# The feed-forward products of a two-layer block as 2x2 blocks with seven products, block sums on GpSimd

## The chip, the cores and the metric

The kernel runs on one core of one Trainium2 chip, in one launch. The metric is the device time in microseconds, as the median of three runs; lower is better. The engines are TensorE (PE; its weight loads are PEld), VectorE (DVE), ScalarE (ACT), GpSimd (POOL) and SyncE (SP), which issues the DMAs.

## What is computed

One sequence of 512 tokens with 1024 features passes two layers of a first block and then one layer of a second block (a sparse attention over compressed, selected and windowed keys). A layer of the first block has a mixer (mLSTM and sliding-window attention) and a feed-forward part, which is what is changed here. All values are float32.

```python
D_MODEL, SEQ, DEPTH, D_FF = 1024, 512, 2, 4096

def sqrelu_mlp(h, w_up, w_down):
    return jnp.square(jax.nn.relu(h @ w_up)) @ w_down

for l in range(DEPTH):
    h = rmsnorm(x, norm_mix_g[l])
    x = x + mixer_block(h, ...)
    h = rmsnorm(x, norm_mlp_g[l])
    x = x + sqrelu_mlp(h, w_up[l], w_down[l])
```

## The kernel before

Activations lie feature-major: a tile holds 128 features on the partitions and all 512 tokens along the free dimension, so 1024 features are eight tiles. To keep float32 accuracy, each operand is split in two parts of the type fp32r, a high part `h` (a rounded copy, made on ScalarE) and a low part `l` (the value less `h`, made on VectorE). A product of two operands is three matmuls: `h*h`, `l*h` and `h*l` (`mm3`).

`gemm` makes one output tile of 128 features and 512 tokens: `wload` fetches one column tile of the weights (128 x 1024, 512 KB) into `raw`, makes `wh` on ScalarE and `wl` on VectorE, and 8 k tiles x 3 matmuls of 512 columns add up in one PSUM bank (tag `g`, four banks). The weights are the stationary operand of each matmul.

In `mlp` the feed-forward part goes in four quarters `qr`. In each, eight up tiles are made from the normed input `xs` (already split, with the norm's gain), then eight down tiles from the eight new hidden tiles `hid`, which are added to the residual `x` in SBUF. The norm's scale per token, `Rb`, multiplies an up tile on its way out of PSUM, in the same instruction as the relu:

```python
self.stt(z, ps, 0.0, Rb, ALU.max, ALU.mult)
self.nc.scalar.activation(z, z, AF.Square)
hid.append(self.split(z, None, "hid"))
```

After the last quarter, `done` is called for each tile: it adds the square of the tile to the statistics of the next norm (`stat_add`: square on ScalarE, sum on GpSimd), spills the tile to DRAM and splits it for the next stage (`prep`). In the second layer a second scaled copy and a second sum of squares are made.

The order of the work is a plan. Every instruction is first recorded in program order (`Recorder`); `issue` then runs a list schedule over the five engines with modelled durations (`cost`), latencies between engines (`LAT`) and the slots of the tile pools, and emits the instructions in that order. Each engine takes its own queue in order. The model has no term for two engines that hinder each other. Pools: `u` (128 x 512 tiles, 79 slots), `raw`, `wh` and `wl` (3 slots each), PSUM banks `g`, `a`, `o`. All instructions are emitted from one line (L306), so the profile's groups are told apart by the tiles' names.

## Time and profile before

| | |
|---|---|
| Runs, median (lowest to highest of 3) | 2189.11 us (2189.09 to 2190.42) |
| Profiled execution, span from first to last instruction | 2187.0 us |
| The time less the span | 2.1 us |
| TensorE busy | 2143.8 us (98%) |
| VectorE, ScalarE, GpSimd busy | 1382.8, 1061.7, 456.8 us |
| Granted clock of TensorE, mean | 0.996 |

The span is that of one profiled execution, the median that of unprofiled runs; what lies around the span is their difference. Matmuls are pipelined: a record's duration is longer than the distance between two starts, so a pace is read from the starts.

### The profile page before, as it was taken

Reading aid. Unit: us, or ns where it says so; the run is one execution under the profiler, and the core shown is the slowest. Engines: PE = TensorE matmul, PEld = TensorE weight load, DVE = VectorE, ACT = ScalarE, POOL = GpSimd, SP = SyncE. Lnnn points to the kernel's source line nnn. Section 1 sums busy time; section 2 is a strip of 40 time slices with the busy share of each in tenths; the row PEclk is TensorE's granted clock in tenths of the full one; section 3 lists DMA queues with packets and bytes.
Section 4 is the critical chain, followed back from the end, with each engine's and each line's share of the span. In section 5 each row is a group of like instructions: output and inputs, shape, how many; then the busy total and the mean of one; then the engine's idle time right before and its main releaser. Section 6 shows DMA issues by size and latency. Waiting matters only on the chain.

```text
span 2187.0 us, 28119 instructions
## 1 busy us (share of the span) xinstructions
PE 2143.8 (98%) x10389; PEld 1766.4 (81%) x10389; DVE 1382.8 (63%) x2591; ACT 1061.7 (49%) x2066; POOL 456.8 (21%) x502
## 2 busy tenths in 40 slices
PE   8999999999999999999999999999999999999998
PEld 6778788887888888887878888788888798888887
DVE  6688995444343445678897445434435677888886
ACT  4466773234232334456675223422324456687783
POOL 3133551012000002014454002000000514232310
PEclk9999999999999999999999999999999999999999
DMA  5223223432333333322322333233333343222321
GB/s 163 77 64 91 75 71 102 130 97 92 97 99 97 97 97 116 97 78 77 88 70 80 112 124 97 87 96 97 98 96 116 97 152 102 69 76 67 90 78 58
DMA packets 72425, 206.10 MB, mean 94 GB/s; under 512 B 9760, under 2 KB 18592, under 8 KB 72288
## 3 DMA queue, kind: packets, MB, share of 16 engines
q1 hardware_dynamic: 72288, 204.31, 30.8%
q8 instruction: 81, 1.33, 0.2%
q14 instruction: 56, 0.46, 0.1%
HBM read 197.86 MB, written 6.42 MB: 93 GB/s over the span
## 4 chain that ended last, share of the span: by engine, by line
PE 79%; DVE 11%; ACT 4%; POOL 3%; issue 2%; DMA 0%; SPq 0%; DVEq 0%; POOLq 0%; ACTq 0%
PE g L306 62%; PE gt L306 6%; DVE L L306 3%; PE O L306 2%; PE PT L306 2%; PE S L306 2%; PE go L306 2%; DVE wl L306 1%; DVE hal L306 1%; PE num L306 1%; ACT L L306 1%; POOL vd L306 1%; ACT wh L306 1%; PE ST L306 1%; POOL sq L306 1%
## 5 line engine op out<-in xcount | busy, mean ns | idle before, releaser
L306 ACT ACTIVATE wh<-raw 128x1024 fp32r<-128x1024 f32 (+2 forms) x344 | 355.4, 1034 | 792.3 <-PE g L306 603.0
L306 PE MATMUL g<-xgh,wh 128*128 128x512 f32 x1512 | 595.6, 394 | 1.9 <-ACT xgh L306 1.7
L306 PE MATMUL g<-xgl,wh 128*128 128x512 f32 x1512 | 595.5, 394 | 0.1
L306 PE MATMUL g<-xgh,wl 128*128 128x512 f32 x1512 | 594.3, 393 | 0.8 <-POOL wl L306 0.8
L306 DVE TENSOR_TENSOR wl<-raw,wh 128x1024 fp32r<-128x1024 f32 (+2 forms) x327 | 406.9, 1245 | 118.0 <-ACT wh L306 117.2
L306 PEld LDWEIGHTS g<-xgh,wh 128*128 128x128 f32 x1512 | 284.7, 188 | 55.4 <-ACT xgh L306 2.7
L306 PEld LDWEIGHTS g<-xgh,wl 128*128 128x128 f32 x1512 | 284.7, 188 | 55.3 <-POOL wl L306 1.2
L306 PEld LDWEIGHTS g<-xgl,wh 128*128 128x128 f32 x1512 | 284.6, 188 | 53.8 <-DVE xgl L306 1.2
L306 POOL TENSOR_TENSOR sq<-sq 128x512 f32<-128x512 f32 x50 | 86.5, 1731 | 596.4 <-ACT sq L306 584.8
L306 PE MATMUL g<-hidh,wh 128*128 128x512 f32 x512 | 199.2, 389 | 0.0
L306 PE MATMUL g<-hidh,wl 128*128 128x512 f32 x512 | 199.2, 389 | 0.0
L306 PE MATMUL g<-hidl,wh 128*128 128x512 f32 x512 | 199.2, 389 | 0.0
L306 DVE TENSOR_TENSOR x<-x,g 128x512 f32<-128x512 f32 x80 | 55.0, 688 | 205.6 <-PE g L306 205.6
L306 DVE SCALAR_TENSOR_TENSOR hz<-g,Rb 128x512 f32<-128x512 f32 x64 | 44.3, 692 | 156.4 <-PE g L306 151.9
L306 ACT ACTIVATE L<-L,mn 128x256 f32<-128x256 f32 (+3 forms) x256 | 131.0, 513 | 17.1 <-DVE mn L306 14.8
L306 PEld LDWEIGHTS g<-hidh,wl 128*128 128x128 f32 x512 | 96.1, 188 | 20.0
L306 PEld LDWEIGHTS g<-hidl,wh 128*128 128x128 f32 x512 | 96.1, 188 | 19.9
L306 PEld LDWEIGHTS g<-hidh,wh 128*128 128x128 f32 x512 | 96.1, 188 | 19.9
L306 PE MATMUL gt<-wh,xgh 128*128 128x512 f32 (+3 forms) x256 | 89.2, 348 | 5.3 <-DVE cf L306 5.3
L306 DVE TENSOR_TENSOR z<-g,Rb 128x512 f32<-128x512 f32 x72 | 49.5, 688 | 65.2 <-PE g L306 64.9
L306 DVE TENSOR_TENSOR pl<-PT,ph 128x512 fp32r<-128x512 f32 (+1 forms) x160 | 79.4, 526 | 16.1 <-ACT ph L306 14.9
L306 PE MATMUL gt<-wh,xgl 128*128 128x512 f32 (+3 forms) x256 | 88.0, 344 | 0.0
(308 smaller groups left out, 3798.3 us busy)
## 6 DMA issues: line engine op xcount, KB each, us to landing
raw<-wf SPq DMA_DIRECT2D x258, 512.0 KB, 3.5
raw<-wn SPq DMA_DIRECT2D x41, 512.0 KB, 3.6
raw<-wmv SPq DMA_DIRECT2D x16, 512.0 KB, 3.6
x<-x SPq DMA_DIRECT2D x16, 256.0 KB, 4.8
bt<-E SPq DMA_DIRECT2D x16, 256.0 KB, 5.0
xsp<-x SPq DMA_DIRECT2D x16, 256.0 KB, 2.0
raw<-w SPq DMA_DIRECT2D x8, 512.0 KB, 3.2
bn<-E SPq DMA_DIRECT2D x16, 256.0 KB, 4.6
```

The costliest lines, as they stand in the source:

```text
L306: op.fn(*op.args, **op.kw)
```

## The change

The feed-forward products are made in blocks of 2 x 2 with seven products in place of eight. A block is two output tiles (features) by two halves of the tokens (256 each), and the sum runs over pairs of k tiles. `wforms` loads two column tiles of weights and makes the seven weight operands: the four GpSimd sums and differences of 512 columns each, then high and low parts by ScalarE and VectorE. `forms` does the same for the right-hand side of a pair of k tiles, with four GpSimd differences of 256 columns. `pair` runs the seven products (each 4 pairs of k tiles x 3 matmuls of 256 columns) into four half banks of PSUM, copies the running value of one of them out three times (ScalarE) and makes the four output blocks from these copies and the other half banks (VectorE).

The norm's scale per token is taken off the up products (relu and square let its square be applied after the down products): `Rb` holds its square and multiplies the sum `y` of the four quarters at the end of `mlp`. For this the down products are collected in `y`, not in `x`; `x` is spilled to DRAM at the end of the mixer and read back in the last quarter. The relu moves to ScalarE. Weights of the feed-forward part get another column order on the host (`_fw`). The pools for weights grow from 3 to 4 slots (`wh`, `wl`) and 5 (`raw`), `u` shrinks from 79 to 78, and a DMA scratch area is made smaller.

```diff
+    def forms(self, b1, b2):
+        nc = self.nc
+        lo, hi = slice(0, 256), slice(256, 512)
+        t, v = self.u("t"), self.u("t")
+        sub = lambda o, x, y: nc.gpsimd.tensor_tensor(o, x, y, op=ALU.subtract)
+        q = self.u("q1", F32R)
+        self.split_to(q[:, lo], q[:, hi], b1[:, lo])
+        b = self.split(b2, None, "q2")
+        sub(v[:, lo], b2[:, hi], b1[:, hi])
+        sub(t[:, lo], b1[:, hi], b1[:, lo])
+        sub(t[:, hi], b2[:, hi], t[:, lo])
+        sub(v[:, hi], t[:, hi], b2[:, lo])
+        t, v = self.split(t, None, "qt"), self.split(v, None, "qv")
+        of = lambda x, s: (x[0][:, s], x[1][:, s])
+        return {1: (q[:, lo], q[:, hi]), 2: of(b, lo), 3: of(b, hi), 4: of(v, hi), 5: of(t, lo), 6: of(t, hi), 7: of(v, lo)}
+    def wforms(self, s1, s2):
+        nc = self.nc
+        lo, hi = slice(0, 512), slice(512, 1024)
+        new = lambda tag: self.nc.tile(self.wp, [128, 1024], F32 if tag == "raw" else F32R, tag, tag, RB if tag == "raw" else WB)
+        r1, r2, s = new("raw"), new("raw"), new("raw")
+        nc.sync.dma_start(r1, s1)
+        nc.sync.dma_start(r2, s2)
+        out = {}
+        def split(x, *ps):
+            h, l = new("wh"), new("wl")
+            n = x.shape[1]
+            self.split_to(h[:, :n], l[:, :n], x)
+            for i, p in enumerate(ps):
+                out[p] = h[:, i * 512:i * 512 + 512], l[:, i * 512:i * 512 + 512]
+        tt = lambda o, x, y, op: nc.gpsimd.tensor_tensor(o, x, y, op=op)
+        split(r1, 1, 2)
+        tt(s[:, lo], r1[:, lo], r2[:, lo], ALU.subtract)
+        tt(r2[:, lo], r2[:, lo], r2[:, hi], ALU.add)
+        split(r2, 5, 4)
+        tt(s[:, hi], r2[:, lo], r1[:, lo], ALU.subtract)
+        split(s, 7, 6)
+        tt(r1[:, hi], r1[:, hi], s[:, hi], ALU.subtract)
+        split(r1[:, hi], 3)
+        return out
+    def pair(self, s1, s2, B, out):
+        A = self.wforms(s1, s2)
+        p, q = self.ps("g", "gp"), self.ps("g", "gq")
+        X, W, Y, Z = p[:, :256], p[:, 256:], q[:, :256], q[:, 256:]
+        sn, sm = self.u("sn"), self.u("sn")
+        a, b, c = sn[:, :256], sn[:, 256:], sm[:, :256]
+        new = set()
+        def mul(o, bank, i, last):
+            h, l = A[i]
+            for j in range(4):
+                s = slice(j * 128, j * 128 + 128)
+                self.mm3(o, (h[:, s], l[:, s]), B[j][i], bank not in new and j == 0, last and j == 3)
+            new.add(bank)
+        snap = lambda o: self.nc.scalar.activation(o, X, AF.Copy)
+        mul(X, 0, 1, False)
+        mul(W, 0, 2, True)
+        snap(a)
+        out(0, a, W, ALU.add)
+        mul(Y, 2, 5, False)
+        mul(Z, 2, 4, True)
+        mul(X, 0, 6, False)
+        snap(b)
+        mul(X, 0, 7, True)
+        snap(c)
+        out(3, c, Y, ALU.add)
+        out(2, c, Z, ALU.subtract)
+        mul(Y, 2, 3, True)
+        out(1, b, Y, ALU.add)
...
-        x, xs, acc = [], [], None
+        B, xg, acc = [], [], None
+        spill = self.dp.tile([128, KT, T], F32, tag="xmid%d" % l, name="xmid")
         for c in range(KT):
             xt = self.u("x")
             nc.sync.dma_start(xt, x_dram[c])
             ps = self.gemm(W(FM_OUT + c), ys)
             self.tt(xt, xt, ps, ALU.add)
-            x.append(xt)
-            xs.append(self.prep(xt, pc[:, PC_GMLP + 8 * l + c:PC_GMLP + 8 * l + c + 1]))
+            nc.sync.dma_start(spill[:, c], xt)
             acc = self.stat_add(acc, xt)
-        return x, xs, acc
+            xg.append(self.u("xg"))
+            nc.scalar.activation(xg[c], xt, AF.Copy, scale=pc[:, PC_GMLP + 8 * l + c:PC_GMLP + 8 * l + c + 1])
+            if c % 2:
+                B.append(self.forms(xg[c - 1], xg[c]))
+        return [spill[:, c] for c in range(KT)], B, acc
...
-    def mlp(self, l, x, xs, acc, done):
-        a = self.a
+    def mlp(self, l, xsp, B, acc, done):
+        nc, a = self.nc, self.a
         W = lambda t: a["wf"][l, t]
         rcol = self.rsqrt(self.stat_sum(acc), 1.0 / D)
-        Rb = self.bcast(rcol)
+        r2 = self.sm("r2", NB)
+        self.tt(r2, rcol, rcol)
+        Rb = self.bcast(r2)
+        y = [None] * KT
+        half = lambda x, n: x[:, n * 256:n * 256 + 256]
+        def combine(z):
+            return lambda n, a, P, op: self.tt(half(z[n // 2], n % 2), a, P, op)
         for qr in range(4):
-            hid = []
-            for t in range(8):
-                ps = self.gemm(W(FM_UP + qr * 8 + t), xs)
-                z = self.u("hz")
-                self.stt(z, ps, 0.0, Rb, ALU.max, ALU.mult)
-                self.nc.scalar.activation(z, z, AF.Square)
-                hid.append(self.split(z, None, "hid"))
-            for c in range(KT):
-                ps = self.gemm(W(FM_DOWN + qr * 8 + c), hid)
-                self.tt(x[c], x[c], ps, ALU.add)
+            H = []
+            for t in range(0, 8, 2):
+                z = self.u("z"), self.u("z")
+                f = FM_UP + qr * 8 + t
+                self.pair(W(f), W(f + 1), B, combine(z))
+                for x in (z[1], z[0]):
+                    nc.scalar.activation(x, x, AF.Relu)
+                    nc.scalar.activation(x, x, AF.Square)
+                H.append(self.forms(*z))
+            for c in range(0, KT, 2):
+                z = self.u("z"), self.u("z")
+                f = FM_DOWN + qr * 8 + c
+                self.pair(W(f), W(f + 1), H, combine(z))
+                for n in (1, 0):
+                    if qr == 0:
+                        y[c + n] = z[n]
+                    else:
+                        self.tt(y[c + n], y[c + n], z[n], ALU.add)
                 if qr == 3:
-                    done(c, x[c])
-
+                    for n in range(2):
+                        xt = self.u("x")
+                        nc.sync.dma_start(xt, xsp[c + n])
+                        self.tt(y[c + n], y[c + n], Rb)
+                        self.tt(xt, xt, y[c + n], ALU.add)
+                        done(c + n, xt)
...
-U_SLOTS, SM_SLOTS, WB, RB = 79, 32, 3, 3
+U_SLOTS, SM_SLOTS, WB, RB = 78, 32, 4, 5
...
+def _fw(w):
+    n = w.shape[1]
+    return w.reshape(4, 2, 128, n // 128, 128).transpose(3, 2, 1, 0, 4).reshape(n // 128, 128, 1024)
...
-        down = [_fm(i["w_down"][l][q * 1024:(q + 1) * 1024]) for q in range(4)]
+        down = [_fw(i["w_down"][l][q * 1024:(q + 1) * 1024]) for q in range(4)]
-                       _fm(i["w_branch_a"][l]), _fm(i["w_out"][l]), _fm(i["w_up"][l])] + down))
+                       _fm(i["w_branch_a"][l]), _fm(i["w_out"][l]), _fw(i["w_up"][l])] + down))
-    nc = bacc.Bacc("TRN2", target_bir_lowering=False, num_devices=1)
+    nc = bacc.Bacc("TRN2", target_bir_lowering=False, num_devices=1, dynamic_dma_scratch_size=1024)
```

## Rows read from the trace of the kernel before

**Rows 1.** The page, parts 1 and 4: busy time, and the chain by engine.
```profile
PE 2143.8 (98%) x10389; PEld 1766.4 (81%) x10389; DVE 1382.8 (63%) x2591; ACT 1061.7 (49%) x2066; POOL 456.8 (21%) x502
...
PE 79%; DVE 11%; ACT 4%; POOL 3%; issue 2%; DMA 0%; SPq 0%; DVEq 0%; POOLq 0%; ACTq 0%
```

**Rows 2.** Stretches, the two feed-forward stages: busy time (instructions), granted clock, DMA share, GB/s.
```profile
529.00:871.00 342.00, 342.00 (x1510) 283.17 (x1510) 152.95 (x167) 112.75 (x143) 11.96 (x8) 1.00 0.32 100
1379.00:1721.00 342.00, 342.00 (x1510) 283.20 (x1509) 154.02 (x165) 121.72 (x157) 20.41 (x15) 1.00 0.33 102
```

**Rows 3.** Waits from 529 to 870 us: us in total, times, longest.
```profile
ACT wh L306 <- PE g L306: 210.8, 58, 4.4
...
DVE hz L306 <- PE g L306: 75.9, 30, 3.1
...
DVE hz L306 <- ACT Rb L306: 2.3, 1, 2.3
```

**Rows 4.** TensorE in order of time, down product: start, us; first and last of 33.
```profile
599.78 0.39 PE L306 MATMUL g<-hidh,wh 128*128 128x512 f32 x1
...
607.04 0.39 PE L306 MATMUL g<-hidl,wh 128*128 128x512 f32 x1
```

**Rows 5.** TensorE in order of time, 256 columns: first and last of 95.
```profile
1797.35 0.28 PE L306 MATMUL gt<-wh,xgl 128*128 128x256 f32 x1
...
1808.61 0.28 PE L306 MATMUL gt<-wl,xgh 128*128 128x256 f32 x1
```

**Rows 6.** Groups by form, ScalarE: busy, mean ns | idle before, releaser.
```profile
L306 ACT ACTIVATE wh<-raw 128x1024 fp32r<-128x1024 f32 x323 | 341.9, 1059 | 763.5 <-PE g L306 589.7 <-issue 142.3 <-PE gt L306 29.7
...
L306 ACT ACTIVATE hidh<-hz 128x512 fp32r<-128x512 f32 x64 | 40.6, 634 | 2.0
...
L306 ACT ACTIVATE ph<-PT 128x256 fp32r<-128x256 f32 x96 | 33.4, 377 | 14.6 <-PE PT L306 14.0
```

**Rows 7.** VectorE in order of time from 841 to 846 us.
```profile
842.48 1.23 DVE L306 TENSOR_TENSOR wl<-raw,wh 128x1024 fp32r<-128x1024 f32 x1 [0.41 <-ACT wh L306]
843.62 1.78 DVE L306 SCALAR_TENSOR_TENSOR xgl<-x,pc,xgh 128x512 fp32r<-128x512 f32 x1
```

**Rows 8.** GpSimd in order of time from 841 to 846 us.
```profile
843.11 1.75 POOL L306 TENSOR_TENSOR sq<-sq 128x512 f32<-128x512 f32 x1 [3.70 <-ACT sq L306]
```

**Rows 9.** Groups by form, VectorE.
```profile
L306 DVE TENSOR_TENSOR hidl<-hz,hidh 128x512 fp32r<-128x512 f32 x64 | 44.4, 693 | 2.8 <-ACT hidh L306 2.7
...
L306 DVE TENSOR_TENSOR pl<-PT,ph 128x256 fp32r<-128x256 f32 x96 | 37.5, 419 | 6.9 <-ACT ph L306 6.2
```

**Rows 10.** The tile sq: duration in ns, min/median/max, first and last start.
```profile
L306 POOL TENSOR_TENSOR sq<-sq x50: 1262/1778/4976, 11.4 to 1724.4; 128x512 f32<-128x512 f32 x50
```

**Rows 11.** VectorE in order of time from 986 to 994.5 us.
```profile
987.39 0.68 DVE L306 TENSOR_TENSOR z<-g,Rb 128x512 f32<-128x512 f32 x1
988.38 1.32 DVE L306 TENSOR_TENSOR wl<-raw,wh 128x1024 fp32r<-128x1024 f32 x1 [0.32 <-ACT wh L306]
989.63 1.23 DVE L306 SCALAR_TENSOR_TENSOR z<-z,num 128x512 f32<-128x512 f32 x1
990.77 1.23 DVE L306 TENSOR_TENSOR nMd<-nMb,maskn 128x512 f32<-128x512 f32 x1
```

**Rows 12.** GpSimd in order of time from 986 to 994.5 us.
```profile
985.60 3.02 POOL L306 TENSOR_TENSOR num<-num,Rm 128x512 f32<-128x512 f32 x2 [2.35 <-ACT Rm L306]
988.59 4.01 POOL L306 TENSOR_TENSOR vd<-v 128x256 f32<-128x256 f32 x3
```

**Rows 13.** The tile wl: duration in ns, min/median/max.
```profile
L306 DVE TENSOR_TENSOR wl<-raw,wh x327: 559/1226/2130, 4.4 to 2083.7; 128x1024 fp32r<-128x1024 f32 x153, 128x512 fp32r<-128x512 f32 x4, 128x528 fp32r<-128x528 f32 x4, 128x608 fp32r<-128x608 f32 x2
```

**Rows 14.** Groups by form, GpSimd.
```profile
L306 POOL TENSOR_TENSOR y<-y,yb 128x256 f32<-128x256 f32 x30 | 23.4, 781 | 28.4 <-DVE y L306 22.7 <-ACT L L306 4.0
```

**Rows 15.** Stretches of 25 us, columns as in rows 2.
```profile
225.00:250.00 25.00, 24.41 (x127) 19.86 (x126) 23.66 (x71) 19.42 (x60) 12.45 (x18) 1.00 0.20 54
1725.00:1750.00 25.00, 19.27 (x91) 14.94 (x90) 18.03 (x38) 6.15 (x11) 14.38 (x27) 0.94 0.16 48
1750.00:1775.00 25.00, 24.22 (x156) 23.18 (x157) 21.66 (x38) 12.73 (x19) 8.56 (x18) 0.93 0.53 168
```

## The prediction

> **What bounds the kernel now.** I read the page first. TensorE is busy for 2143.8 of 2187.0 us and takes 79% of the chain that ended last [rows 1], so the end is set by how fast matmuls follow each other, and by whatever keeps them waiting. The runs have a median of 2189.1 us, 2.1 us above the profiled span; I add that 2.1 us unchanged, so differences of the span are differences of the time.
>
> Then the table of stretches over the two feed-forward stages: 342.0 of 342.0 us busy on TensorE in each, while VectorE works 153 us, ScalarE 113 and GpSimd 12 [rows 2]. The table of waits in the first of them shows only engines that wait for matmuls [rows 3]. So the stage is bound by the matmul pace and the others have air. The pace is the distance between starts, not the 0.39 us of one record: from 599.78 to 607.04 us there are 32 steps, so 0.2269 us for 512 columns [rows 4]. A layer has 64 output tiles of 24 matmuls; both layers 3072, or 697.0 us. I count in pairs of output tiles: 64 pairs of 48 matmuls, 10.89 us each.
>
> **TensorE's part of the change.** A pair becomes 7 products x 4 pairs of k tiles x 3 = 84 matmuls of 256 columns, each with its own weight load. The trace has such a stream, a token-major product with 256 columns: 94 steps from 1797.35 to 1808.61 us, so 0.1198 us each [rows 5], a little more than half of 0.2269. A pair costs 10.06 us, 64 pairs 643.8 us: TensorE gains 53.2 us, not the eighth of 697 (87 us) that counting columns would give. That gain is kept only if the other engines deliver a pair in 10.06 us.
>
> **What the other engines must do for a pair.** Weights: four GpSimd sums of 512 columns; high parts on ScalarE, low parts on VectorE, three of 1024 columns and one of 512. Right-hand side (an up pair only): four GpSimd differences of 256 columns, four low parts on VectorE (one of 256, three of 512). Recombination: three ScalarE copies and four VectorE sums of 256 columns that read PSUM.
>
> ScalarE for an up pair: three 1024-column casts at 1.06 us, one half and two-block work at 0.63 us a piece (one weight cast, three casts, four relu and square), one cast of 256 and three copies at 0.38 [rows 6]: 3.2 + 5.0 + 1.5 = 9.7 us. It fits under 10.06, barely.
>
> VectorE and GpSimd each fit alone as well, but they don't run side by side. At 842.48 us VectorE begins a weight subtraction that reads two SBUF tensors and ends at 843.71; GpSimd's sum, begun at 843.11, ends only at 844.86, 1.15 us after VectorE's end; VectorE's next, begun at 843.62, ends at 845.40, 0.54 us after GpSimd's [rows 7, 8]. With nothing beside them a VectorE subtraction of 512 columns takes 0.69 us [rows 9] and that GpSimd sum 1.26 at the least [rows 10]. So they take turns, and a turn costs 1.15 us for 512 columns on GpSimd and 0.54 on VectorE. The dense stretch at 986 us gives the rest: GpSimd's pair of products ends at 988.62 and VectorE's 1024-column subtraction at 989.70, a turn of 1.08 us; two VectorE turns of 512 columns, with one of GpSimd's 256-column differences between them, end at 990.86 and 992.00, 1.14 us apart, which leaves 0.60 us for the difference [rows 11, 12]. A VectorE operation that takes one operand from PSUM keeps its 0.68 us in the middle of a GpSimd product (987.39 us) [rows 11]: the recombining sums need no turn. For 256 columns on VectorE I take 0.28 us, half of 0.54 (an estimate).
>
> Turns for the weights of a pair: 4 x 1.15 + 3 x 1.08 + 0.54 = 8.38 us. For a right-hand side: 4 x 0.60 + 0.28 + 3 x 0.54 = 4.30 us. **An up pair needs 12.68 us of turns**, over 10.06 and over the old 10.89. A down pair needs 8.38, and 9.46 with the two additions into y of quarters 1 to 3; TensorE bounds it at 10.06. In quarter 3 each tile adds the scale, the residual and a low part on VectorE and GpSimd's sum of squares: 3 x 0.54 + 1.15 = 2.77 us in the first layer, so 15.0 us a pair; the second layer has another GpSimd sum, 17.3 us.
>
> The weights' buffers (four slots for high and low parts, and a pair uses four) let the engines run less than a pair ahead, so a down pair's spare 0.6 us pays little for the up pairs. Sum: 32 x 12.68 + 24 x 10.06 + 4 x 15.0 + 4 x 17.3 = 405.8 + 241.4 + 129.2 = 776.4 us against 697.0: **+79.4 us** with every turn taken without a gap. If all slack could be shared, the turns alone would be 405.8 + 8 x 8.38 + 16 x 9.46 + 129.2 = 753.4, +56.4 us: the lower bound.
>
> By the Trainium skill, SBUF — State Buffer, section "Who interferes with whom", a VectorE instruction with two SBUF inputs and a GpSimd instruction that reads SBUF exclude each other for a whole instruction, and one with a single SBUF input doesn't contend. The trace agrees on who blocks whom, but not on the length: 0.54 of VectorE's 0.69 us count. By the whole lengths an up pair would be 15.0 us instead of 12.68; that is the second rival below.
>
> **What comes on top.** VectorE takes its queue in order: when a subtraction at its head waits for a turn, the PSUM sums behind it wait too. Four at 0.42 us recorded [rows 9], some 0.33 back to back, are 1.3 us a pair; between all hidden and none I take half, 0.65 us over the 40 pairs that turns bound: +26 us (0 to 52).
>
> Joins: the first down products of a quarter need the right-hand side of the last up tiles: PSUM sum 0.42, relu and square 1.25, four differences 2.4, cast and low part 1.3, so 5.4 us and more with contention. TensorE can go on with the other three k pairs of four products, 36 matmuls or 4.3 us; 1.1 us is left, 8 joins: +9 us (0 to 45 if each difference must also let a 1.08 us subtraction by). Ahead of the stage the same chain from the residual: +1 us twice. Behind it two tiles now end at once, each with sum, scale, residual and split ahead of the next stage's matmuls: some 2.5 us more than the one old tile, twice: +5 us.
>
> The rest costs nothing here: the spill of the residual and its reload are 32 transfers of 256 KB on SP's queue, needed only a quarter of a stage later, with the DMA engines at 0.32 [rows 2]; were one late, the residual addition of quarter 3 would wait and with it VectorE's queue, and the weight loads that stand behind it on SP's queue with it. The token scale is no longer needed at the start; it gives back at most the 2.3 us that VectorE once waited [rows 3], not TensorE's.
>
> 79.4 + 26 + 9 + 2 + 5 = 121 us: 2187 + 121 + 2 = **2310 us**. This case's own range is 2245 (lower bound, nothing on top) to 2395 (all tops at their upper ends, 79 + 52 + 45 + 7 = 183, and some 20 for turns that nobody takes).
>
> **Rivals.**
> *TensorE stays the bound* (the other side). If VectorE and GpSimd overlapped enough, the stage would be 643.8 us plus joins and ends of 16: 2189 - 53 + 16 = 2152 us. It decides from the point where an up pair's turns fall below 10.06 us, that is 2.6 of GpSimd's 7.0 us hidden behind VectorE. For it: from 225 to 250 us VectorE is busy for 23.7 us and GpSimd for 12.5, and TensorE still for 24.4 [rows 15]. Against it: every overlap that I followed was a turn [rows 7, 8, 11, 12]. Chance 0.09. Overlap in part, with a time from 2185 to 2245: 0.05.
>
> *Each turn costs the whole instruction.* With recorded durations (1.23, 0.69 and 0.42 on VectorE [rows 9, 13], 1.26 and 0.78 on GpSimd [rows 10, 14]) an up pair is 6.9 + 8.2 = 15.0 us, a down pair 10.8, quarter 3 about 17.5 and 20.0: 480 + 259 + 150 = 889, +192, with joins and ends 2397 us. For it: durations are what an engine shows when nothing follows at once. Against it: 0.54 us after GpSimd's end [rows 7, 8]. Chance 0.09. It is the rule of the skill's SBUF page taken by the letter.
>
> *The clock falls.* TensorE would idle about a fifth of each up pair. After the stalls at 1725 us the granted clock was 0.94 and 0.93 over two stretches [rows 15], part of them at the lower of its two levels; in the old stage it was 1.00 [rows 2]. At 0.93 a pair takes 10.8 us, which costs 24 x 0.75 = 18 us in down pairs and nothing in up pairs. It decides below 0.79 (10.06 / 12.68); at 0.75 a pair is 13.4 us and the time about 2189 + 56 x 13.4 + 129 - 697 + 42 = 2413 us. [...] Chance 0.05. The Trainium skill, TensorE: Matmul & The Clock Gate, Part 1, says that the gate stands at half rate unless activity releases it; no run shown here has a stage with TensorE at 80%.
>
> **Chances.** Turns bound the stage: 0.72, predicted 2310. The range 2240 to 2415 holds that case, nearly all of the whole-instruction and half of the clock case: 0.81. A measurement of this kernel tells about 0.2%, 4.4 us, from no change. Faster 0.10 (first rival and a little of the partial one), same 0.02, slower 0.88.
>
> **What would show it.** In the profile after: matmuls of 256 columns 0.12 us apart within a product; TensorE near 80% in up stretches, waiting for the high or low part of a weight, and fuller in down stretches; VectorE with GpSimd filling 95% between them; GpSimd's 512-column sums at 1.7 us or more and VectorE's 1024-column subtractions stretched above 1.23 us. An up pair near 13 us and a down pair near 10.5 confirm the sum; an up pair at 10 to 11 us refutes the turns. I would be wrong if the schedule places GpSimd's work where VectorE reads PSUM or waits, or if ScalarE at 9.7 us, in order, becomes the engine that the others wait for.

## The result, and the profile after

The changed kernel takes **2358.3 us** (median of four runs, 2356.0 to 2360.9) against 2189.1: a ratio of 1.077 [1.076, 1.079]. It is slower, as forecast, and 48 us above the forecast of 2310; the time lies inside the range of the likeliest case. The profiled span is 2354.2 us, 167.2 longer than before. The two feed-forward stages hold nearly all of it. From the first up matmul to the end of the last down matmul they take 432.6 + 432.3 = 864.9 us, against 350.9 + 350.9 = 701.8 before; the 697.0 of the prediction is their matmuls' pace alone, without the waits in between. The rest of the program is some 4 us longer, and the first stage begins 4 us later. These are the first and last matmuls of the two stages before:

```profile
517.67 0.39 PE L306 MATMUL g<-xgh,wh 128*128 128x512 f32 x1
868.15 0.39 PE L306 MATMUL g<-hidl,wh 128*128 128x512 f32 x1
...
1366.69 0.39 PE L306 MATMUL g<-xgh,wh 128*128 128x512 f32 x1
1717.20 0.39 PE L306 MATMUL g<-hidl,wh 128*128 128x512 f32 x1
```

The profile page's busy times after the change come first, then the table of stretches over the two stages (busy time of TensorE, its weight loads, VectorE, ScalarE and GpSimd, each with its instructions; granted clock; DMA share; GB/s).

```profile
PE 2182.1 (93%) x12693; PEld 1887.6 (80%) x12693; DVE 1758.9 (75%) x3009; ACT 1306.5 (55%) x2546; POOL 1047.5 (44%) x918
```
```profile
521.60:954.20 432.60, 370.68 (x2712) 351.49 (x2711) 329.87 (x371) 231.38 (x375) 291.53 (x200) 0.93 0.28 89
1451.80:1884.10 432.30, 370.42 (x2718) 350.77 (x2717) 331.39 (x370) 238.64 (x387) 296.01 (x203) 0.93 0.28 91
```

Against [rows 2], TensorE now idles for 62 of 432 us, VectorE and GpSimd both work through most of the stage, and the granted clock has gone from 1.00 to 0.93. The matmuls themselves are as quick as predicted where nothing holds them up. TensorE in order of time (start, duration) in a down pair, 0.12 us from start to start:

```profile
719.82 0.28 PE L306 MATMUL gq<-q2h,wl 128*128 128x256 f32 x1
719.94 0.28 PE L306 MATMUL gq<-q2l,wh 128*128 128x256 f32 x1
720.06 0.28 PE L306 MATMUL gq<-qvh,wl 128*128 128x256 f32 x1
720.18 0.28 PE L306 MATMUL gq<-qvl,wh 128*128 128x256 f32 x1
```

Where the time lies inside a quarter comes out when the starts of every 84th such matmul are taken as marks, one pair of output tiles apart. In quarter 1 of the first layer the eight pairs last 11.0, 11.0, 12.8, 15.0 (up) and 20.8, 10.6, 10.7, 10.7 us (down), 102.6 in all, where the kernel before took 10.89 for each, 87.1 in all. The other quarters show the same figure: the first pair of a stage takes 20.3 and 19.3 us, every first down pair 20.5 to 20.8, and the last two pairs of a stage 18.3 and 14.6 in the first layer, 19.2 and 15.7 in the second. The same quarter as stretches: up pairs, first down pair, other down pairs; then the up pairs apart, the first two together, the third, the fourth.

```profile
634.40:684.20 49.80, 44.28 (x338) 42.34 (x337) 40.30 (x42) 30.07 (x51) 37.40 (x26) 0.97 0.27 86
684.20:705.00 20.80, 14.54 (x87) 13.20 (x86) 12.23 (x14) 10.48 (x18) 11.55 (x12) 0.75 0.15 50
705.00:737.00 32.00, 31.23 (x254) 30.48 (x253) 24.77 (x30) 14.07 (x22) 21.89 (x13) 1.00 0.31 99
...
634.40:656.40 22.00, 20.67 (x171) 20.26 (x170) 16.61 (x18) 12.05 (x20) 14.03 (x9) 1.00 0.32 98
656.40:669.20 12.80, 11.07 (x86) 10.26 (x85) 11.30 (x13) 9.84 (x17) 11.08 (x10) 1.00 0.24 82
669.20:684.20 15.00, 12.55 (x86) 11.81 (x85) 12.39 (x13) 8.19 (x16) 12.29 (x9) 0.89 0.22 71
```

In the up pairs VectorE and GpSimd record 77.7 us in a stretch of 49.8. That is no sign that they work side by side, since a record can hold the wait for its turn. In the first two pairs TensorE is nearly full; in the third and fourth VectorE and GpSimd are, and TensorE isn't. The groups by form (busy us, mean ns of one | idle before) show how far they are stretched, against 1262 ns for a GpSimd sum at its shortest [rows 10]:

```profile
L306 POOL TENSOR_TENSOR raw<-raw 128x512 f32<-128x512 f32 x256 | 418.1, 1637 | 200.9 <-DVE wl L306 191.1 <-DMA raw<-wf 3.2
...
L306 DVE TENSOR_TENSOR wl<-raw,wh 128x1024 fp32r<-128x1024 f32 x370 | 539.9, 1465 | 181.5 <-ACT wh L306 178.4
```

The first down pair is another matter. It has the lowest clock, 0.75, and no engine is busy for three quarters of it. Three views in order of time show what it waits for (idle time before an instruction, and its releaser, in brackets): TensorE, VectorE, and the two engines that feed them.

```profile
684.46 0.28 PE L306 MATMUL gq<-qtl,wh 128*128 128x256 f32 x1
687.91 0.39 PE L306 MATMUL gq<-qth,wh 128*128 128x256 f32 x1 [3.17 <-ACT qth L306]
689.03 0.58 PE L306 MATMUL gq<-qtl,wh 128*128 128x256 f32 x1 [0.62 <-DVE qtl L306]
689.69 0.58 PE L306 MATMUL gq<-q2h,wh 128*128 128x256 f32 x1
...
692.21 0.41 PE L306 MATMUL gq<-q2l,wh 128*128 128x256 f32 x1
694.97 0.58 PE L306 MATMUL gp<-q,wh 128*128 128x256 f32 x1 [2.35 <-ACT q L306]
...
698.54 0.31 PE L306 MATMUL gq<-qth,wh 128*128 128x256 f32 x1
```
```profile
687.89 1.09 DVE L306 TENSOR_TENSOR qtl<-t,qth 128x512 fp32r<-128x512 f32 x1 [1.28 <-ACT qth L306]
688.90 0.74 DVE L306 TENSOR_TENSOR z<-sn,gq 128x256 f32<-128x256 f32 x2
...
692.66 0.42 DVE L306 TENSOR_TENSOR z<-sn,gq 128x256 f32<-128x256 f32 x1 [1.30 <-PE gq L306]
...
697.65 0.69 DVE L306 TENSOR_TENSOR qtl<-t,qth 128x512 fp32r<-128x512 f32 x1 [2.10 <-ACT qth L306]
```
```profile
681.71 2.59 POOL L306 TENSOR_TENSOR t<-z 128x256 f32<-128x256 f32 x2
684.27 1.27 POOL L306 TENSOR_TENSOR raw<-raw 128x512 f32<-128x512 f32 x1
685.49 1.71 POOL L306 TENSOR_TENSOR t<-z,t 128x256 f32<-128x256 f32 x1
...
694.55 1.59 POOL L306 TENSOR_TENSOR t<-z 128x256 f32<-128x256 f32 x2 [3.74 <-ACT z L306]
```
```profile
693.19 1.27 ACT L306 ACTIVATE z<-z 128x512 f32<-128x512 f32 x2
694.50 0.42 ACT L306 ACTIVATE q<-z 128x256 fp32r<-128x256 f32 x1
696.98 0.63 ACT L306 ACTIVATE qth<-t 128x512 fp32r<-128x512 f32 x1 [2.07 <-POOL t L306]
```

Read it backwards. The last product of the up half is the twelve matmuls from 689.69 us. It couldn't start before VectorE's sum at 688.90, and that sum stands in VectorE's queue behind the low part qtl at 687.89. That one belongs to the right-hand side of the pair before, and waited for ScalarE's cast, which waited for GpSimd's differences: from 681.71 to 687.20 GpSimd makes three of them, with a weight sum among them. The down matmuls that should fill a gap (those from the first three right-hand sides) stood ahead of this product in TensorE's queue and were spent by 689.6, with a wait of 3.2 us of their own. When the last product ends at 692.6, the chain of sum, relu and square, differences, cast and low part begins anew and ends at 698.3 with little left to run under it. After the waits matmuls start 0.21 us apart, not 0.12: in the granted clock's terms part of this pair ran at the lower of the two levels, as its mean of 0.75 says. The Trainium skill, TensorE: Matmul & The Clock Gate, Part 1, has TensorE at half rate unless activity releases it; this stretch agrees. The waits weigh more than the clock: over the eight first down pairs 60 steps of more than 0.26 us from start to start make up 65 us above the pace of 0.12, and 205 steps of 0.19 to 0.26 us make up 19.5.

The stage as a ledger, in us for both layers, by the terms of the forecast's sum (measured against forecast):

| term | measured | forecast | difference |
|---|---|---|---|
| 32 up pairs, without the entry | 396.9 | 32 x (12.68 + 0.65) = 426.6 | -30 |
| entry of the two stages | 17.5 | 2 | +16 |
| first down pairs above 10.06, 8 joins | 85 | 9 | **+76** |
| other down pairs of quarters 0 to 2 (18) | 193.8 | 181.1 | +13 |
| quarter 3's down pairs (its first at 10.06) | 111.4 | 134.4 | -23 |
| all else, against 2187.0 - 697.0 | -0.7 | 5 | -6 |

The entry is what the first pair of a stage takes above 11.0 us. The first down pairs of quarters 0 to 2 stand in neither column with their 10.06 us. The last row sets the program without its stages against the old one without the stages' pace, as the forecast did; the 4.8 us by which the old stages were longer than their pace lie in it. The differences add to 46 us, the distance between the profiled span and the forecast one (2354.2 - 2308). So one term carries the miss, the joins, and with it the entry, where the first up products wait for the right-hand sides of the last residual tiles. With the sums on VectorE (below) the first pair of a stage falls from 20.3 and 19.3 us to 12.7.

### The profile page after: what moved, and what is told of

It reads as the page before. It is cut to its first block, busy times and chain, and to the rows that moved or that the text cites. A ratio compares the mean times of both kernels' runs of the same rounds, so it can differ in the third digit from the quotient of the medians.

```text
span 2354.2 us, 34576 instructions
## 1 busy us (share of the span) xinstructions
PE 2182.1 (93%) x12693; PEld 1887.6 (80%) x12693; DVE 1758.9 (75%) x3009; ACT 1306.5 (55%) x2546; POOL 1047.5 (44%) x918
## 3 DMA queue, kind: packets, MB, share of 16 engines
q8 instruction: 100, 1.64, 0.3%
## 5 line engine op out<-in xcount | busy, mean ns | idle before, releaser
L306 ACT ACTIVATE wh<-raw 128x1024 fp32r<-128x1024 f32 (+1 forms) x472 | 462.1, 980 | 559.4 <-PE g L306 171.1
L306 DVE TENSOR_TENSOR wl<-raw,wh 128x1024 fp32r<-128x1024 f32 (+1 forms) x455 | 629.5, 1389 | 183.5 <-ACT wh L306 180.2
L306 POOL TENSOR_TENSOR raw<-raw 128x512 f32<-128x512 f32 x256 | 418.1, 1637 | 200.9 <-DVE wl L306 191.1
L306 PE MATMUL g<-xgh,wh 128*128 128x512 f32 x1000 | 395.4, 396 | 3.2 <-ACT xgh L306 3.0
L306 PE MATMUL g<-xgl,wh 128*128 128x512 f32 x1000 | 395.8, 396 | 0.7 <-DVE xgl L306 0.5
L306 PE MATMUL g<-xgh,wl 128*128 128x512 f32 x1000 | 395.0, 395 | 0.6 <-DVE wl L306 0.6
L306 PEld LDWEIGHTS g<-xgh,wh 128*128 128x128 f32 x1000 | 188.5, 189 | 37.6 <-ACT xgh L306 4.5
L306 PEld LDWEIGHTS g<-xgl,wh 128*128 128x128 f32 x1000 | 188.6, 189 | 35.8 <-DVE xgl L306 2.8
L306 PEld LDWEIGHTS g<-xgh,wl 128*128 128x128 f32 x1000 | 188.5, 189 | 34.8 <-DVE wl L306 1.0
L306 ACT ACTIVATE L<-L,mn 128x256 f32<-128x256 f32 (+3 forms) x256 | 131.1, 514 | 25.7 <-DVE mn L306 23.2
L306 PE MATMUL gp<-q,wh 128*128 128x256 f32 x512 | 118.5, 297 | 25.9 <-ACT q L306 18.8
L306 ACT ACTIVATE z<-z 128x512 f32<-128x512 f32 (+1 forms) x177 | 109.6, 619 | 15.7 <-DVE z L306 13.9
L306 PEld LDWEIGHTS gp<-q,wh 128*128 128x128 f32 x512 | 88.0, 194 | 35.2 <-ACT q L306 21.7
L306 DVE TENSOR_TENSOR pl<-PT,ph 128x512 fp32r<-128x512 f32 (+1 forms) x160 | 79.5, 525 | 21.8 <-ACT ph L306 20.5
```

The lines of the kernel that those rows point to most:

```text
L306: op.fn(*op.args, **op.kw)
```

## The experiments

Every run is set against a run of the kernel before on the same chip; times are medians, of two runs where the edit changes the values and of four or five elsewhere. Pair times are those of quarter 1 of the first layer, found as above.

**Do GpSimd's reads cost the time?** Each of GpSimd's sums becomes two memsets of the same tile, so that it works and signals much as before but reads nothing. An instruction that reads nothing also has fewer others to wait for: the four differences of a right-hand side no longer depend on each other.

```diff
-        tt = lambda o, x, y, op: nc.gpsimd.tensor_tensor(o, x, y, op=op)
+        def tt(o, x, y, op):
+            for _ in range(2):
+                nc.gpsimd.memset(o, 0.5)
...
-        sub(v[:, lo], b2[:, hi], b1[:, hi])
-        sub(t[:, lo], b1[:, hi], b1[:, lo])
-        sub(t[:, hi], b2[:, hi], t[:, lo])
-        sub(v[:, hi], t[:, hi], b2[:, lo])
-        t, v = self.split(t, None, "qt"), self.split(v, None, "qv")
+        for x in (b2[:, hi], b1[:, hi], b1[:, lo], b2[:, lo]):
+            for _ in range(2):
+                nc.gpsimd.memset(x, 0.5)
+        t, v = self.split(b1, None, "qt"), self.split(b2, None, "qv")
```


> GpSimd's place in the changed kernel stays, but it reads nothing: each of its sums and differences is replaced by two memsets of the same columns (values differ from the reference's). For the right-hand side they write into the hidden tiles themselves, behind the square, so that the splits still wait for GpSimd. Two memsets of 512 columns are about 1.07 us and of 256 about 0.64, close to a turn's 1.15 and 0.60. Turns theory (GpSimd's reads exclude VectorE's two-input instructions): VectorE's 1024-column low parts fall back to 1.23 us, up pairs to 10.1 to 10.6, only the joins remain; 2215 to 2255, like the kernel with the sums on VectorE. If GpSimd's slowness and its place in the chain are the cost, without exclusion: 2310 or more.

Measured 2241.95 us, 1.024 [1.022, 1.026]: 116 us less than the change. Stretches of up pairs, first down pair and other down pairs, and two groups by form:

```profile
617.80:660.00 42.20, 40.98 (x339) 40.54 (x338) 28.60 (x43) 30.27 (x52) 20.94 (x55) 1.00 0.30 101
660.00:676.50 16.50, 12.50 (x86) 11.79 (x85) 8.70 (x13) 9.38 (x16) 8.05 (x21) 0.90 0.21 65
676.50:707.10 30.60, 30.60 (x254) 30.41 (x254) 20.79 (x30) 14.47 (x22) 10.68 (x23) 1.00 0.32 103
```
```profile
L306 DVE TENSOR_TENSOR wl<-raw,wh 128x1024 fp32r<-128x1024 f32 x370 | 474.4, 1285 | 242.1 <-ACT wh L306 237.1 <-DMA raw<-wf 1.0 <-DMA x<-x 0.5
L306 POOL MEMSET raw<- 128x512 f32 x512 | 256.3, 525 | 315.2 <-DVE wl L306 264.4 <-DMA raw<-wf 44.1 <-issue 0.7
```

VectorE's subtraction is back at 1285 ns from 1465, and the four up pairs take 42.2 us instead of 49.8. GpSimd still has two instructions of 0.53 us for each sum, nearly as long as a sum alone (1.26), so in the up pairs it isn't its work in itself but what it reads. The Trainium skill, SBUF — State Buffer, "Who interferes with whom", has VectorE undisturbed by a GpSimd instruction that only writes; these 1285 ns agree. The memset has another cost in the planner's table than the sum, so the order may differ in places. Part of the 116 us is a shorter join: the first down pair falls from 20.8 to 16.5 us.

**The same sums on VectorE.** All block sums and differences move from GpSimd to VectorE, which then works alone.

```diff
-        sub = lambda o, x, y: nc.gpsimd.tensor_tensor(o, x, y, op=ALU.subtract)
+        sub = lambda o, x, y: nc.vector.tensor_tensor(o, x, y, op=ALU.subtract)
...
-        tt = lambda o, x, y, op: nc.gpsimd.tensor_tensor(o, x, y, op=op)
+        tt = lambda o, x, y, op: nc.vector.tensor_tensor(o, x, y, op=op)
```


> All sums and differences of the blocks run on VectorE, nothing else changed. Turns theory: no turns are left but those of the statistics; VectorE works 7.1 us of low parts, 1.3 of PSUM sums and 3.3 of block sums in an up pair, 11.7 us, and about 8.3 in a down pair, so about 2240 us, 2210 to 2280. If instead GpSimd's help is worth more than its turns cost, VectorE becomes a worse bound and the time is above 2358.

Measured 2246.4 us, 1.026 [1.024, 1.027]; pairs of 10.1, 10.4, 11.2, 12.8 up and 15.0, 10.1, 10.1, 10.1 down. Stretches as above:

```profile
615.40:659.80 44.40, 41.78 (x338) 40.67 (x337) 40.98 (x70) 31.72 (x54) 0.00 (x0) 1.00 0.29 96
659.80:674.80 15.00, 12.20 (x86) 11.60 (x85) 13.86 (x24) 8.39 (x14) 0.00 (x0) 0.89 0.21 70
674.80:705.10 30.30, 30.30 (x255) 30.30 (x254) 28.38 (x44) 14.23 (x22) 0.00 (x0) 1.00 0.33 105
```

One engine, busy for 41.0 us, gets through an up half in 44.4 where two took 49.8, and the first down pair is 5.8 us shorter. With nothing of the computation left out, this is 112 us less than the change: what the sums cost on GpSimd over VectorE. It isn't all turns in the up pairs. Between the two profiled executions (109.5 us apart) the up pairs with the entries get shorter by 57 us, the first down pairs by 43 and the other down pairs of quarters 0 to 2 by 11, while quarter 3's get longer by 4.

**The joins alone.** Down products take the right-hand sides of the up half (B), which are long there, instead of H: the same matmuls, sums and turns, but no down product waits for the up half of its quarter.

```diff
-                self.pair(W(f), W(f + 1), H, combine(z))
+                self.pair(W(f), W(f + 1), B, combine(z))
```


> The down products take the up products' right-hand side, which is there from the start, in place of the hidden tiles' (values differ from the reference's). Every instruction of the changed kernel stays, GpSimd's included; only TensorE's wait for the last hidden tiles at the 8 joins is cut. Turns theory: turns bound the up pairs at 12.7 us and more, quarters of 89 to 93 us, 2260 to 2300. Joins theory (the waits at the joins are the main loss, and turns matter little between them): quarters of 81 to 87 us, 2190 to 2245.

Measured 2322.4 us, 1.061 [1.059, 1.063]: 36 us less than the change, and above what either theory gave. Quarter 1: 11.0, 11.0, 12.8, 14.0 and 13.5, 16.2, 10.6, 10.9.

```profile
626.00:674.90 48.90, 43.57 (x339) 42.16 (x338) 39.83 (x42) 29.68 (x50) 36.48 (x25) 0.97 0.25 87
674.90:688.30 13.40, 10.63 (x85) 10.19 (x85) 10.51 (x13) 8.76 (x15) 9.47 (x9) 1.00 0.23 78
688.30:726.00 37.70, 33.70 (x255) 33.11 (x254) 29.69 (x33) 15.47 (x24) 23.29 (x17) 0.91 0.25 84
```

The up half is as slow as in the change (48.9 against 49.8), so the turns are untouched. The first down pair falls to 13.4 us, but the second rises to 16.2: the last two up pairs' sums and differences are still to be done in turns, and TensorE probably meets that backlog a pair later; over both layers the first down pairs get shorter by 52 us and the other down pairs longer by 28. A part of what I had put to the joins is therefore probably the turns of the right-hand sides, which fall due there.

**Both at once**, the sums on VectorE and the down products from B.

> The fourth corner: all block sums on VectorE (no turns) and the down products taken from the up products' right-hand side (no joins; values differ from the reference's); every instruction of the kernel with VectorE's sums stays. Joins theory: the 7 to 8 us that the fourth up pair and the first down pair of each quarter cost above 10.1 go, 8 x 7.5 = 60 us, so 2175 to 2195, with the closing pairs of quarter 3 still above 15. If VectorE itself holds the up pairs at 11.7 us once the joins no longer give it air: 2225 to 2250.

Measured 2217.1 us, 1.013 [1.010, 1.016], between the two expectations. Quarter 1: 10.1, 10.1, 10.7, 12.3 and 10.8, 11.2, 10.1, 10.6. The table of stretches across the join:

```profile
650.00:700.00 50.00, 49.02 (x400) 48.01 (x399) 47.78 (x77) 26.27 (x41) 0.00 (x0) 1.00 0.30 101
```

With neither GpSimd's sums nor joins the clock is at 1.00 and TensorE busy for 98% of these 50 us, but VectorE for 96%: the quarters before the last still take some 86 us where 8 x 10.06 would be 80.5, as VectorE alone is nearly the bound. The four kernels make a square:

| | joins kept | joins cut | what the joins cost |
|---|---|---|---|
| sums on GpSimd | 2358.3 | 2322.4 | 36 |
| sums on VectorE | 2246.4 | 2217.1 | 29 |
| what the sums cost on GpSimd over VectorE | 112 | 105 | 141 together |

The two causes add, within 7 us, and leave 2217 against 2189 - 53 = 2136 for a stage that TensorE alone bounds.

**Which sums matter?** First the weights' sums left out, then the right-hand sides' differences left out.

```diff
-        r1, r2, s = new("raw"), new("raw"), new("raw")
+        r1, r2 = new("raw"), new("raw")
...
         split(r1, 1, 2)
-        tt(s[:, lo], r1[:, lo], r2[:, lo], ALU.subtract)
-        tt(r2[:, lo], r2[:, lo], r2[:, hi], ALU.add)
         split(r2, 5, 4)
-        tt(s[:, hi], r2[:, lo], r1[:, lo], ALU.subtract)
-        split(s, 7, 6)
-        tt(r1[:, hi], r1[:, hi], s[:, hi], ALU.subtract)
+        split(r2, 7, 6)
         split(r1[:, hi], 3)
```


> The four GpSimd sums over the weights of each pair are left out, and the seven weight operands are cut from the two raw tiles as they are (values differ from the reference's); every matmul, split, PSUM sum and the differences of the right-hand side stay. Turns theory (VectorE and GpSimd exclude each other): an up pair's turns fall from 12.7 to 8.1 us, below TensorE's 10.06, and the differences at the joins have fewer turns to wait for; 2165 us, between 2150 and 2200. Order theory (the plan's order, made with durations that know no turns, makes TensorE wait at the joins whatever the load): most of the waits in the third and fourth up pair and the first down pair stay, 2240 to 2300. Chain theory (the join is long because its steps depend on each other): pairs at 10.1 to 10.6 but each join still 6 us or more above its 10 us, 2190 to 2230.

```diff
...
-        sub(v[:, lo], b2[:, hi], b1[:, hi])
-        sub(t[:, lo], b1[:, hi], b1[:, lo])
-        sub(t[:, hi], b2[:, hi], t[:, lo])
-        sub(v[:, hi], t[:, hi], b2[:, lo])
-        t, v = self.split(t, None, "qt"), self.split(v, None, "qv")
+        t, v = self.split(b1, None, "qt"), self.split(b2, None, "qv")
```


> The four GpSimd differences of each right-hand side are left out and the two input tiles are split in their place (values differ from the reference's); the weights' sums stay. Turns theory: an up pair needs 10.3 us of turns, about TensorE's 10.06, and the closing pairs still 15 to 17; 2190 to 2230 us. Chain theory: the join loses four of its ten steps, 2.4 us of them at the least and some 9 us with what stands between them in GpSimd's queue; the first down pair falls from 20.7 to 12 us or so, also about 2200, but then with up pairs of quarter 1 unchanged at 11. Order theory: 2300 or more.

Without the weights' sums 2260.3 us, 1.032 [1.030, 1.034]; without the differences 2282.5, 1.042 [1.040, 1.044]. The second fits none of its expectations. The first missed the 2165 that the turns were to give and lies in the range of the order theory. Its stretches speak for the chain, which came out longer than its range allowed:

```profile
619.70:661.70 42.00, 40.85 (x339) 40.47 (x338) 28.97 (x42) 29.84 (x51) 8.42 (x10) 1.00 0.32 101
661.70:681.90 20.20, 14.65 (x86) 13.61 (x86) 10.20 (x14) 10.55 (x18) 5.38 (x6) 0.75 0.17 52
681.90:712.10 30.20, 30.20 (x254) 30.20 (x254) 20.80 (x30) 14.12 (x22) 0.00 (x0) 1.00 0.33 105
```

The up pairs are at 10.1, 10.1, 10.3 and 11.5 us and the other down pairs at 10.1, and the first down pair is as long as in the change, 20.2 us at a clock of 0.75. So the join doesn't come from too much work: GpSimd is busy for 5.4 of these 20.2 us and VectorE for 10.2. It is the length of the chain, with the low clock beside it. Where GpSimd doesn't make the differences, the same pair takes 15.0 (on VectorE), 16.0 (left out) and 16.5 us (memsets).

**Is it only the order?** Four attempts at the schedule. The planner's costs of two-input instructions are raised on both engines (e4, the first two edits below); the first down pair's matmuls are held behind the last of the up half (e7, the next two), and the same with the sums on VectorE (e8); or the previous pair's differences are recorded in the middle of the next pair (e10, the last edit).

```diff
-            return 69 + n / (1.92 if fast else 0.96) + 61 * scalars
+            two = len([x for x in ins if not _psum(x)]) > 1
+            return 69 + n / (1.92 if fast else 0.96) * (1.3 if two else 1) + 61 * scalars
...
-            return (108 + 2.18 * n) if kw.get("op") != ALU.pow else 230 + 183 * n
+            return (108 + 3.4 * n) if kw.get("op") != ALU.pow else 230 + 183 * n
...
+        if eng == PE and self.gate is not None:
+            preds.setdefault(self.gate, False)
...
+                nc.gate = max(i for i, op in enumerate(nc.ops) if op.eng == PE) if c == 0 else None
...
-                self.pair(W(f), W(f + 1), B, combine(z))
+                self.pair(W(f), W(f + 1), B, combine(z), (lambda: H.append(self.forms(*last))) if last else None)
```


> The same instructions as the changed kernel in another order: in the planner's model GpSimd's operations last 3.4 instead of 2.18 ns a column, and VectorE's with two SBUF inputs 1.3 times as long. Order theory: TensorE's queue no longer stands early down products ahead of late up products, joins fall by half, 2270 to 2310 us. Turns theory: the turns remain and only their place changes, 2320 to 2360. No effect of the order: within 10 us of 2358.

> The changed kernel with one more rule in the plan: no down matmul of a quarter stands in TensorE's queue ahead of the last matmul of that quarter's last up pair. No instruction changes. Order theory: the last up product no longer waits behind early down products, the first down pair falls from 20.7 to 13 or 14 us; 2300 to 2315. If the chain of dependent steps behind the last up product, on slowed engines, is the join: within 15 us of 2358, either way, since early down matmuls no longer fill the waits for weights.

> The same rule in the plan on top of all block sums on VectorE, so without turns. Order theory: the first down pair falls from 15 to 11 or 12 us and the fourth up pair from 12.8 to 11; 2200 to 2215. No effect of the order: 2235 to 2255.

> The changed kernel with one more rule in the plan: VectorE's four low parts of an up pair's right-hand side stand in its queue behind the two PSUM sums of the next pair that free the bank for that pair's last product. No instruction changes. Queue theory (in the third and fourth up pair TensorE waits for a PSUM sum that stands on VectorE behind a low part, which waits for GpSimd): these pairs fall from 12.8 and 15.0 us to 11 or so, the first down pair stays at 20; 2300 to 2325. Turns theory without a part for the queue: the work moves but its sum stays, 2345 to 2370.

| kernel | us | ratio |
|---|---|---|
| e4 | 2349.2 | 1.073 [1.071, 1.074] |
| e7 | 2356.2 | 1.076 [1.074, 1.078] |
| e8 | 2235.9 | 1.021 [1.020, 1.022] |
| e10 | 2361.0 | 1.078 [1.077, 1.080] |

None is worth more than 11 us (e8 is to be set against the 2246.4 with the sums on VectorE). In e4 the first down pair even grows, to 23.4 us. In e7 the last up pair takes 23.2 us and the first down pair 12.0, together 35.2 where the change has 35.8. TensorE in order of time:

```profile
688.48 0.58 PE L309 MATMUL gq<-q2h,wh 128*128 128x256 f32 x1 [6.00 <-DVE z L309]
```

The last up product now shows its wait openly, 6.0 us for VectorE's PSUM sum, while the down matmuls are kept for the chain behind it. The wait has moved, no more: there are two chains in a row, the one before the last product and the one behind it, and cover for one of them. That the cover was spent in the wrong place is thus no cause by itself. In e10 the differences come earlier, and the third up pair pays for it (14.4 to 16.9 us).

**A version that beats both kernels.** The up half alone by blocks, with the sums on VectorE; its two hidden tiles are split as before the change and the down half is the old 24 matmuls of 512 columns. There are no differences of hidden tiles, and so no chain of them at the joins.

```diff
-                H.append(self.forms(*z))
...
+                for x in z:
+                    H.append(self.split(x, None, "hid"))
+            for c in range(KT):
+                ps = self.gemm(W(FM_DOWN + qr * 8 + c), H)
...
```


> Seven products for the up half alone, block sums on VectorE; the down half as before the change, 48 matmuls of 512 columns a pair from split hidden tiles, summed in y. There are no differences of hidden tiles, so the joins are as short as before and VectorE works some 10 us in an up pair. TensorE: 32 pairs of 10.06 and 32 of 10.89, 25 us less than before the change; less some 10 for the start of the stage and the closing tiles: 2165 to 2180, which would be faster than before. If VectorE, with 3.8 + 2.2 + 1.3 + 1.1 us a pair and in order, holds the weights up: 2190 to 2210.

Measured 2180.1 us (2178.4 to 2180.8 in five runs), 0.9955 [0.9943, 0.9968]: some 9 us faster than before, at the upper edge of the expected range. It is a small gain, but outside its interval. Stretches of the two stages:

```profile
521.30:860.30 339.00, 338.43 (x2124) 306.61 (x2123) 222.28 (x302) 179.08 (x270) 10.91 (x10) 1.00 0.35 114
1361.70:1701.60 339.90, 338.90 (x2124) 306.80 (x2123) 223.46 (x298) 184.94 (x278) 15.72 (x12) 1.00 0.35 114
```

TensorE is full again at a clock of 1.00, and the stages take 678.9 us against 701.8: 23 us won, where half of TensorE's saving would be 26.6. Some 15 of the 23 are lost again outside the stages, which take 1500.0 us instead of 1485.2: the first layer's out-projection, for one, starts at 477.7 us instead of 474.1. A further step put relu and scale into one VectorE instruction and kept the residual in SBUF:

```diff
+                    self.stt(x, x, 0.0, Rb, ALU.max, ALU.mult)
...
+                self.tt(x[c], x[c], ps, ALU.add)
```


> Seven products for the up half alone, block sums on VectorE, and the rest as before the change: the token scale is multiplied in with the relu (VectorE, two SBUF inputs) and the residual stays in SBUF. Against the first such kernel (2180) the closing tiles lose a multiplication and an addition each and the next stage starts as it did before the change: 2168 to 2177. If the scale on VectorE (2 x 0.69 us an up pair on top of some 8.5) makes the low parts late: 2180 to 2195.

It gave 2180.4 us, 0.9954 [0.9940, 0.9968], the same as the kernel without this step, and above the 2168 to 2177 that I had expected. Its stages take 686.3 us and all else 1492.3, so what it won outside the stages it lost inside them. What holds up the program outside the stages was not isolated.

## Why the prediction was right and wrong

The direction and the main mechanism were right. That the time fell within 48 us of the forecast is in part luck: the joins, the entries and the other down pairs cost 105 us more than their terms, while the up pairs, quarter 3 and all else cost 59 less.

**TensorE's part was right.** 0.12 us a matmul, and 30.2 us for three undisturbed down pairs (10.07 each) in the run without weight sums.

**The turns were right as a cause; their size agrees in part only.** With TensorE as the bound in place of turns the forecast was 2152 us, so it charged the turns, with the PSUM sums held up by them, with 158 us. Taking GpSimd's reads away gave 116 us, moving the sums to VectorE 112, or 105 with the joins cut, and both of the first two hold a part of the joins. (The 79.4 + 26 = 105 of the forecast is the rise over the old pace, so it can't be set against these.) The length of a turn fits where turns fill a pair: the third up pair takes 12.8 us, with VectorE recorded for 11.3 and GpSimd for 11.1 of them, against 12.68 forecast and 15.0 by whole instructions; the up half as a whole takes 49.8 against 50.7. But the pairs aren't even: 11.0, 11.0, 12.8, 15.0. In the first two TensorE is busy for 20.67 of 22.0 us, so turns don't bound them, and by my own sign, "an up pair at 10 to 11 us refutes the turns", they alone would have spoken against me. Probably each quarter begins with some work already done and ends with right-hand sides due. The 0.65 us for PSUM sums isn't there in the mean of the up pairs (12.4, where 13.33 was expected), and quarter 3's pairs were dear by 23 us in the forecast: there the engines probably use waits that I had counted as lost. Down pairs of quarters 0 to 2, at 10.06 in the forecast, came at 10.77 (193.8 / 18); where GpSimd's reads are gone they are at 10.1 to 10.2 on average, so their turns weigh too.

**The step that failed is the joins**, "1.1 us is left, 8 joins: +9 us (0 to 45 ...)", and with it "ahead of the stage the same chain from the residual: +1 us twice". The chain itself was sized well: 5.7 us from the end of the last up product (692.6) to the low part (698.3), against 5.4. Wrong was what stands around it. First, there are two such chains in a row, because the last up product must wait for a PSUM sum that is queued on VectorE behind a low part of the right-hand side before, and that comes through GpSimd; the 36 matmuls that I set against one chain cover neither whole. Second, matmuls after such waits start 0.21 us apart instead of 0.12. Measured, a join costs 10.6 us and not 1.1, and the eight together 85, outside the term's own range of 0 to 45. Of the 85 us in the first down pairs 42 are left when VectorE makes the sums, 33 when the dependence is cut, and 9 with both; in quarter 1 the pair falls from 20.8 us to 15.0, 13.5 and 10.8. By the square of four kernels the dependence alone is worth 29 to 36 us of the time. The forecast had both ingredients of this, the in-order queue of VectorE and the run-ahead of less than a pair, and used neither at the join.

**The clock fell beside the turns, not instead of them.** I held the fall for a rival (0.05) with 0.93 as its mild form; the stages' mean is 0.93 indeed. In the records of both stages 476 steps from matmul to matmul lie between 0.19 and 0.26 us; at 0.12 they would have been some 46 us shorter. In the first down pairs such steps account for 19.5 of the 85 us, and longer waits for the rest. How much of the 46 us the end sees was not separated (in an up pair TensorE might have waited anyway), since no run changed the clock without changing the waits. Where such waits are gone (the stretch across the join with joins cut and sums on VectorE; the stages of the up-only kernel) the clock is 1.00.

**The other rivals.** TensorE as the bound (2152 us) is out: even without GpSimd's sums and without joins the time is 2217. ScalarE, which I had named as a possible bound at 9.7 us, isn't one: 30.1 of 49.8 us in the up pairs. Of the signs that I named, "VectorE with GpSimd filling 95% between them" can't be read from busy times, as records that hold a wait for a turn add to 156% here; the pair times are the sign that works. And TensorE was to wait "for the high or low part of a weight". Its waits in the first layer's stage (us in total, times, longest) are for other things:

```profile
PE gq L306 <- DVE z L306: 20.8, 24, 2.3
PE gq L306 <- ACT qth L306: 12.9, 5, 3.2
...
PE gp L306 <- DVE wl L306: 2.6, 6, 1.3
```

The PSUM sums that stand behind held instructions in VectorE's queue are what it waits for most, and after them the right-hand sides. The forecast named these sums as a cost, but not as the wait through which the turns reach TensorE.

## What to carry to other kernels

A second elementwise engine is only a second engine where its operands don't contend: GpSimd's sums beside VectorE's two-input subtractions cost 112 us here that VectorE alone doesn't pay, so add up the turns of both as if they were one engine. Saved matmuls are worth their measured pace (0.120 us for 256 columns against 0.227 for 512 makes 92% out of seven eighths), and the scheme paid only where the block sums of the right-hand side are made once and early, in the up half alone (0.45% faster). Where one half of a stage feeds the other, follow the last product's chain backwards through every in-order queue until an instruction that waits for nothing, and only then count the cover.

## What the runs showed of the hardware

- GpSimd instructions that write only leave VectorE's two-input subtraction at 1285 ns (1024 columns), as in the up-only kernel (1280), where GpSimd makes no block sums; beside GpSimd's two-input sums the mean is 1465.
- VectorE makes a 512-column sum in 0.69 us and GpSimd in 1.26 at its shortest [rows 9, 10], 1.64 on average here.
- Waits of 2 to 3.5 us with bursts of matmuls between them left a granted clock of 0.75 over 20.8 us (first down pair), while the up pairs of the same quarter, 89% busy, had 0.97.
